# Last phase of a hybrid decoder block: finished rows scaled on ScalarE and GpSimd, gates in own buffers, later mean products, and projection matmuls of 512 columns

## The chip, the cores and the metric

The kernel runs on one core of a Trainium2 chip. The metric is the device time of one execution in microseconds; the time of a kernel is the median of its runs. TensorE (PE) multiplies, with its weight loads (PEld) beside; VectorE (DVE), ScalarE (ACT) and GpSimd (POOL) do the rest, and all transfers here are issued by SyncE (SP), in order.

## The reference

One decoder block with two token mixers over 2048 tokens of 1024 channels, in float32, cut to what matters here:

```python
h = _rmsnorm(x, norm_g) * (1 + scale) + shift
p = h @ w_in                       # c_val, c_gate, c_og, r/k/v/loras, r_og, g_conv, g_rwkv
y_conv = (silu(LN(conv31(c_val * sigmoid(c_gate)))) * silu(c_og)) @ w_conv_out
y_rwkv = (groupnorm(rwkv7_scan(...)) + bonus) * silu(r_og) @ w_rwkv_out
m = sigmoid(g_conv) * y_conv + sigmoid(g_rwkv) * y_rwkv
x = x + gate * (m @ w_out)
return _rmsnorm(x, final_g)
```

## The kernel before, in words

**Number format.** Each product that must be exact to float32 is made of three fp32r matmuls: both operands are split into a high part (a cast on ScalarE) and a low part (a subtraction, on VectorE or GpSimd), and hi x hi, hi x lo and lo x hi are added up in PSUM. `mm3k` (L316) writes the three for one of the eight 128-row slices of the contraction. A result tile is 128 channels x 512 tokens; `MS` (L44) says into how many matmuls its 512 columns are divided, two here, each with its own weight load.

**Stages.** Tokens go in four blocks of 512. The main phase makes, for each block, 73 tiles of the input projection (`product`, L959), the convolution (31 multiply-adds on VectorE, L997), and the delta-rule scan in eight pairs of heads (`pair`, `group`, `inverse`, `merge`), whose 128x512 matmuls L616 to L622 share TensorE's queue with the projections. It leaves convolution rows `y`, scan rows `o`, and the gates (tanh values in `gr_d`, `gc_d`) in DRAM. The last phase begins at about 2283 us and runs for each block `pb` through 8 tiles of the scan branch's output (`rjob`), 8 of the convolution's (`cjob`), and the output product (`ojob`, four column blocks `cb`).

**Beside them** run side chains. `z_first` adds and gates scan rows. `lnorm_first` makes the channel layer norm of `y`: part 0 adds up eight tiles (L1050), then a product with a matrix of ones gives the mean (L1060); part 1 subtracts it (L1069), squares (L1071) and adds (L1078), then a product gives the variance (L1086); part 2 normalises, multiplies by the gate and stores `u` (L1088 to L1107). Some of their operations go to `other()`: GpSimd, or VectorE once all convolution rows of the kernel are made. `hprep` loads `z` or `u` rows and splits them for the next stage (L492, L493).

**The take of a tile.** In `rjob`, L1304 reads a finished PSUM tile with the gate `rth` into `mr`; in `cjob`, L1318 and L1319 do so for the other branch, and L1336 and L1337 split the sum for `ojob`. There are two PSUM buffers for these tiles, so a product's matmuls wait until the take of the second tile before it is done. The gate lies in a ring of two buffers (`t2`), which it shares with the squares of `ojob` (L1380).

**The end of a block.** In `ojob`, L1379 adds the x rows, L1381 sums squares, and `norm` makes the reciprocal root in twelve small VectorE operations and then scales: eight L1392 for a block, VectorE, each followed by a store to `out` (L1394). The tiles of x that are scaled are used again: block 0's by the `mr` tiles of block 1, the others' by the x rows of the next block. Weights of the last phase come split from DRAM, or raw (`raw`, L285 to L291) with the split made on the spot: for the scan branch in blocks 2 and 3, for the convolution branch in blocks 1 to 3.

**Order.** PE's order is written by a planner: each matmul adds its planned time to a clock, jobs follow one another, and threads (side chains, scan) come in when their condition holds and a delay has passed (`yield (condition, delay)`). `late_free` asks whether the one PSUM bank of the side chains is free. The other engines' instructions are put in order by the framework, from its own estimate of times; `tc.high_priority` moves some forward.

Of the kernel before, what the change touches and what calls it, by code (L numbers as in the profile page):

```python
# [9 lines left out]
F32 = mybir.dt.float32  # L10
F32R = mybir.dt.float32r
I32 = mybir.dt.int32
AF = mybir.ActivationFunctionType
ALU = mybir.AluOpType
# [4 lines left out]
P = 128  # L19
D = 1024  # L20
KT = D // P
TB = 512
NTT = TB // P
CH = 64
NCH = TB // CH
# [5 lines left out]
BKB, T2B, OCB = 1, 2, 2  # L31
# [9 lines left out]
OE, LE, CE = 0, 0, 1  # L41
WLL = 1
TRE = 1
MS, MS2 = 2, 1  # L44
WB = 7
OPAD, MOFF = 64, 16
KEPT = ("in",)
# [24 lines left out]
LLD, LST, LDA, LLA, LPO, LDT, LAS, LT1 = 8.0, 3.0, 4.0, 5.0, 36.0, 5.0, 6.0, 3.0  # L72
LOOK, DUO, NHF, LHF, LYJ = 13, 2, 9, 5.0, 34.0
LOOK3, LSD = 80, 2.6
NPB = 4
# [14 lines left out]
def hybrid_block(ctx: ExitStack, tc: tile.TileContext, x, vecs, convk, w2a2, final_g, ada, w_in, w_co, w_ro, w_o, crow, out,  # L90
                 seq=2048, groups=(0, 1, 2, 3), phase2=True, dbg=None):
    nc = tc.nc
# [187 lines left out]
    def load_w(name, n, hl=None, held=None, raw=False):  # L280
        if hl is None:
            hl = [whl.tile([P, KT, P], F32R, name=n_, tag="w", bufs=WB) for n_ in ("w_hi", "w_lo")]
        hi, lo = hl
        back = kept.get((name, n))
        if raw:  # L285
            st = l3.tile([P, KT, P], F32, name="w_raw", tag="tk", bufs=TKB)
            nc.sync.dma_start(st, wsrc[name][n])
            with tc.high_priority(HP):
                nc.scalar.copy(hi, st)
                (nc.gpsimd if name == "ro" and n < 2 else nc.vector).tensor_tensor(out=lo, in0=st, in1=hi.bitcast(F32), op=ALU.subtract)  # L290
            return hi, lo  # L291
        if back is not None:
            nc.sync.dma_start(hi.bitcast(F32), back[0].bitcast(F32))
            nc.sync.dma_start(lo.bitcast(F32), back[1].bitcast(F32))
            return hi, lo
        st = whl.tile([P, KT, P], F32, name="w_st", tag="w", bufs=WB)
        ada_ld[0] = nc.sync.dma_start(st, wsrc[name][n]).ins
        wcount[0] -= 1
        with tc.high_priority(HP):
            nc.scalar.copy(hi, st)  # L300
            lo_eng = nc.vector if wcount[0] >= 0 or (wcount[0] < -1000 and wcount[0] % 4 < W2) else nc.gpsimd
            lo_eng.tensor_tensor(out=lo, in0=st, in1=hi.bitcast(F32), op=ALU.subtract)  # L302
        if name in KEPT:
            i = "_".join(str(k) for k in (n if isinstance(n, tuple) else (n,)))
            def store():
                kept[(name, n)] = [dp.tile([P, KT, P], F32R, name=f"k{p_}_{name}{i}", tag=f"k{p_}_{name}{i}") for p_ in "hl"]
                nc.sync.dma_start(kept[(name, n)][0].bitcast(F32), hi.bitcast(F32))
                nc.sync.dma_start(kept[(name, n)][1].bitcast(F32), lo.bitcast(F32))

            if held is None:  # L310
                store()
            else:
                held.append(store)
        return hi, lo
# [59 lines left out]
    e1 = early.enter_context(tc.tile_pool(name="e1", bufs=1, side="right"))  # L374
    xp = early.enter_context(tc.tile_pool(name="xp", bufs=HXB, side="right"))
    hp = early.enter_context(tc.tile_pool(name="hp", bufs=1, side="right"))
    e2 = early.enter_context(tc.tile_pool(name="e2", bufs=2, side="right"))
# [658 lines left out]
    def lnorm_first(pb, part):  # L1036

        def yload(j):
            yj = hx("lny")
            behind(nc.sync.dma_start(yj, y_dram[pb][j]))  # L1040
            return yj

        if part == 0:
            yield (free, 1.0)
            ys, n_ = yload(0), [yload(1), yload(2)]
            yield LLD
            for j in range(1, KT):
                yield (free, 0.0)
                item(1)
                behind(other().tensor_tensor(out=ys, in0=ys, in1=n_.pop(0), op=ALU.add))  # L1050
                if j + 2 < KT:
                    n_.append(yload(j + 2))
                yield pace(LSD)
                item(-1)
            ln0["ys"] = ys
        elif part == 1:
            n_ = [yload(0)]
            yield (late_free, 0.0)
            ps = pl.tile([P, TB], F32, name="late", tag="late")
            te(0.9).matmul(ps, ones, ln0["ys"], start=True, stop=True)  # L1060
            bank[0] = clock[0] + LCH
            ln0["mean"] = ln0["ys"]
            nc.scalar.copy(ln0["mean"], ps)
            yield LLD
            for j in range(KT):
                yield (free, 0.0)
                item(1)
                yj = n_.pop(0)
                behind(nc.gpsimd.tensor_tensor(out=yj, in0=yj, in1=ln0["mean"], op=ALU.subtract))  # L1069
                yield pace(1.5)  # L1070
                behind(nc.scalar.activation(yj, yj, AF.Square))  # L1071
                if j + 1 < KT:
                    n_.append(yload(j + 1))
                yield pace(1.5)
                if j == 0:
                    qs = yj
                else:
                    behind(other().tensor_tensor(out=qs, in0=qs, in1=yj, op=ALU.add))  # L1078
                yield pace(LSD / 2)
                item(-1)  # L1080
            ln0["qs"] = qs
        else:
            qs = ln0["qs"]
            yield (late_free, 0.0)
            ps = pl.tile([P, TB], F32, name="late", tag="late")
            te(0.9).matmul(ps, ones, qs, start=True, stop=True)  # L1086
            bank[0] = clock[0] + LCH
            nc.vector.tensor_scalar(out=qs, in0=ps, scalar1=LN_EPS, scalar2=None, op0=ALU.add)  # L1088
            ln0["rl"] = hx("lnr")
            rsqrt(ln0["rl"], qs, None, nc.vector, hx("lnt"))  # L1090
            n_ = [yload(0)]
            yield LLD
            for j in range(KT):
                yield (free, 0.0)
                item(1)
                yj, ct = n_.pop(0), hx("lnc")
                behind(nc.sync.dma_start(ct, co_dram[pb][j]))
                behind(nc.gpsimd.tensor_tensor(out=yj, in0=yj, in1=ln0["mean"], op=ALU.subtract))  # L1098
                other().tensor_tensor(out=yj, in0=yj, in1=ln0["rl"], op=ALU.mult)
                yield pace(LST)  # L1100
                swish_y(yj, hx("lnth"), j)
                if j + 1 < KT:
                    n_.append(yload(j + 1))
                yield pace(LST)
                behind(other().tensor_tensor(out=yj, in0=yj, in1=ct, op=ALU.mult))
                yield pace(LST)
                behind(nc.sync.dma_start(u_dram[pb][j], yj))  # L1107
                item(-1)
# [183 lines left out]
    w4 = {}  # L1292
    mtags = ["M", "ta", "E2", "k", "sq", "r", "sh", "lw"]

    def whole(name):
        return l3.tile([P, 2, 2, NCH, P], F32R, name=name, tag="As", bufs=2).rearrange(
            "p q h c t -> p (q h) (c t)").rearrange("p a (b t) -> p (a b) t", t=TB)

    def rjob(b, n):
        def take(ppr):  # L1300
            mr0 = w4.setdefault(("mr", b), [])
            mr0.append(e1.tile([P, TB], F32, name="mr0", tag=mtags[n]))
            with tc.high_priority(HP):
                nc.vector.scalar_tensor_tensor(out=mr0[n], in0=w4.pop(("th", n)), scalar=1.0, in1=ppr, op0=ALU.add, op1=ALU.mult)  # L1304

        def run():
            w4["th", n] = th = e2.tile([P, TB], F32, name="rth0", tag="t2", bufs=T2B)
            nc.sync.dma_start(th, gr_dram[b][n])
            yield from product(n, take, -1000, "ro", b > 1)

        return [None, run(), 0]

    def cjob(b, n):
# [25 lines left out]
            m0[1].append(lo)  # L1339

        def run():
            w4["th", n] = th = e2.tile([P, TB], F32, name="cth0", tag="t2", bufs=T2B)
            nc.sync.dma_start(th, gc_dram[b][n])
            yield from product(n, take, -1000, "co", b > 0)

# [17 lines left out]
    def ojob(b, cb):  # L1363
# [19 lines left out]
        def norm(t0, t1):  # L1383
            ts_ = slice(t0, t1)
            nc.vector.tensor_reduce(out=vs[:, ts_], in_=sq4[:, ts_], axis=AX.X, op=ALU.add)
            nc.vector.tensor_scalar(out=vs[:, ts_], in0=vs[:, ts_], scalar1=1.0 / D, scalar2=RMS_EPS, op0=ALU.mult, op1=ALU.add)
            rsqrt(rs[:, ts_], vs[:, ts_], None, nc.vector, rt[:, ts_])
            for tt in range(t0, t1):
                for half in range(2):
                    hs = slice(half * TB, half * TB + TB)  # L1390
                    xt = xts0[4 * half + tt]
                    nc.vector.scalar_tensor_tensor(out=xt, in0=xt, scalar=rs[:, tt:tt + 1], in1=w4["fg"][:, hs],  # L1392
                                                   op0=ALU.mult, op1=ALU.mult)
                    nc.sync.dma_start(out[b * TB + tt * P:b * TB + tt * P + P, hs], xt)  # L1394

        for kh, tt in [(kh, tt) for tt in range(NTT) for kh in range(2)] if end else [(kh, tt) for kh in range(2) for tt in range(NTT)]:
# [129 lines left out]
```

## Time and profile before

| | us |
|---|---|
| median of 3 runs | 2896.63 (2895.95 to 2897.0) |
| the profiled execution | 2893.5 |
| its span, first to last instruction | 2891.8 |
| PE busy in it, weight loads | 2767.5, 2677.1 |
| VectorE, GpSimd, ScalarE busy | 1998.4, 1338.6, 1017.5 |
| mean granted TensorE clock | 0.986 |

The profile is of one execution. Rows of groups have: line, engine, operation, tiles written and read, shapes, count, then the busy time in all and the mean in ns of one, then the idle time of the engine just before them and what ended it. Rows of the timeline have the start and the length in us, and idle time ahead of the row in brackets. Rows by stage have the stretch, its length, busy time (and count) of PE, PEld, DVE, ACT and POOL, the granted clock, the DMA engines' share and GB/s.

### The profile page before, as it was taken

The numbers are of one execution on the slowest core, as the hardware profiler recorded it, in microseconds if no ns is written. First come the engines' busy times: TensorE is split into PE (matmuls) and PEld (weight loads), VectorE is DVE, ScalarE is ACT, GpSimd is POOL, SyncE is SP. The second block draws the span as 40 slices with busy tenths as digits, with TensorE's granted clock in tenths as the row PEclk, the third lists the DMA queues.
The fourth block names the chain that finished last, engine by engine and source line by source line (L and its number), as shares of the span: only waits on it lengthen the run. The fifth ranks groups of instructions, "written<-read, shape, count | busy, mean of one in ns | idle before, by whom it ended". The sixth has DMA issues, their size and how long they took to land.

```text
span 2891.8 us, 67549 instructions
## 1 busy us (share of the span) xinstructions
PE 2767.5 (96%) x27184; PEld 2677.1 (93%) x27184; DVE 1998.4 (69%) x3453; ACT 1017.5 (35%) x1994; POOL 1338.6 (46%) x1996
## 2 busy tenths in 40 slices
PE   6989999999999999999999999999999999998998
PEld 6988999899999999999999988999999989898998
DVE  6694886767677787768587768586857465666353
ACT  5443334433433324343333343324332233333221
POOL 2447554843555344556455746676665440230000
PEclk9999999999999999999999999999999999999999
DMA  8776877766887776868886667866696779797664
GB/s 316 261 254 216 282 248 243 262 226 216 278 281 250 262 259 199 285 213 252 272 250 212 219 203 225 304 213 229 218 309 206 244 245 331 258 345 261 208 215 161
DMA packets 376971, 717.75 MB, mean 248 GB/s; under 512 B 130833, under 2 KB 149585, under 8 KB 376658
## 3 DMA queue, kind: packets, MB, share of 16 engines
q1 hardware_dynamic: 376658, 713.44, 73.4%
q8 instruction: 214, 3.51, 0.5%
q14 instruction: 99, 0.81, 0.1%
HBM read 511.91 MB, written 200.29 MB: 246 GB/s over the span
## 4 chain that ended last, share of the span: by engine, by line
PE 58%; DVE 11%; DMA 7%; POOL 4%; issue 2%; ACT 1%; SPq 1%; DVEq 0%; POOLq 0%; ACTq 0%
PE ps_main L323 41%; DVE acc L997 3%; PE pout L1403 2%; PE pout L1405 2%; PE pout L1404 2%; PE xo L882 2%; DMA lny<-y_d 2%; PE xo L876 1%; PE aux L692 1%; PE xo L889 1%; DMA w_st<-w_in_t 1%; DMA As<-dT 1%; POOL TT L776 1%; POOL itmp L772 1%; DVE h_lo L493 1%
## 5 line engine op out<-in xcount | busy, mean ns | idle before, releaser
L323 PE MATMUL ps_main<-h_hi,w_hi 128*128 128x256 f32 x5632 | 1173.5, 290 | 29.7 <-DVE mr L1304 13.8
L323 PE MATMUL ps_main<-h_hi,w_lo 128*128 128x256 f32 x5632 | 1111.7, 279 | 2.7 <-POOL w_lo L302 2.1
L323 PE MATMUL ps_main<-h_lo,w_hi 128*128 128x256 f32 x5632 | 1112.8, 279 | 0.0
L323 PEld LDWEIGHTS ps_main<-h_hi,w_hi 128*128 128x128 f32 x5632 | 862.2, 190 | 61.0 <-DVE mr L1304 8.5
L323 PEld LDWEIGHTS ps_main<-h_hi,w_lo 128*128 128x128 f32 x5632 | 860.1, 190 | 3.3 <-POOL w_lo L302 2.6
L323 PEld LDWEIGHTS ps_main<-h_lo,w_hi 128*128 128x128 f32 x5632 | 862.5, 190 | 0.0
L997 DVE SCALAR_TENSOR_TENSOR acc<-u,ck,acc 128x512 f32<-128x512 f32 x928 | 698.4, 753 | 19.5
L772 POOL TENSOR_TENSOR itmp<-La,TT 128x126 f32<-128x126 f32 (+22 forms) x496 | 190.4, 384 | 68.4 <-DMA La<-dA 35.6
L776 POOL TENSOR_TENSOR TT<-TT,itmp 128x126 f32<-128x126 f32 (+22 forms) x496 | 197.2, 398 | 34.6
L302 POOL TENSOR_TENSOR w_lo<-w_st,w_hi 128x1024 fp32r<-128x1024 f32 x51 | 123.6, 2424 | 183.9 <-ACT w_hi L300 170.4
L893 DVE TENSOR_TENSOR S<-xo,Se 64x128 f32<-64x128 f32 x256 | 73.4, 287 | 138.7 <-PE xo L889 131.6
L871 ACT ACTIVATE Se<-S,pe 128x128 f32<-128x128 f32 x256 | 88.9, 395 | 223.1 <-DVE S L893 222.1
L1403 PE MATMUL pout<-w_hi,m_hi 128*128 128x256 f32 x512 | 145.1, 283 | 1.0 <-DVE xt L1379 1.0
L1404 PE MATMUL pout<-w_lo,m_hi 128*128 128x256 f32 x512 | 143.9, 281 | 0.0
L1405 PE MATMUL pout<-w_hi,m_lo 128*128 128x256 f32 x512 | 143.9, 281 | 0.0
L300 ACT CAST w_hi<-w_st 128x1024 fp32r<-128x1024 f32 x71 | 74.4, 1048 | 166.0 <-DMA w_st<-w_in_t 127.3
L884 DVE TENSOR_TENSOR uv<-xo,rn 64x256 f32<-64x256 f32 x128 | 53.7, 420 | 103.5 <-PE xo L882 101.9
L493 DVE TENSOR_TENSOR h_lo<-hf,h_hi 128x512 fp32r<-128x512 f32 x96 | 78.0, 829 | 64.0 <-ACT h_hi L492 63.8
L660 POOL TENSOR_TENSOR ta<-ta,k 128x512 f32<-128x512 f32 x32 | 46.4, 1449 | 131.5 <-ACT ta L659 131.4
L575 ACT ACTIVATE t<-ps_main,mu 128x512 f32<-128x512 f32 x96 | 65.6, 684 | 114.9 <-PE ps_main L323 112.6
L1098 POOL TENSOR_TENSOR lny<-lny 128x512 f32<-128x512 f32 x32 | 45.0, 1407 | 116.2 <-DMA lny<-y_d 87.8
L1403 PEld LDWEIGHTS pout<-w_hi,m_hi 128*128 128x128 f32 x512 | 96.5, 189 | 1.7 <-DVE xt L1379 1.4
(257 smaller groups left out, 4247.9 us busy)
## 6 DMA issues: line engine op xcount, KB each, us to landing
w_hi<-kh_in SPq DMA_DIRECT2D x219, 512.0 KB, 5.6
w_lo<-kl_in SPq DMA_DIRECT2D x219, 512.0 KB, 4.1
w_st<-w_in_t SPq DMA_DIRECT2D x73, 512.0 KB, 4.7
kh_in<-w_hi SPq DMA_DIRECT2D x71, 512.0 KB, 2.9
kl_in<-w_lo SPq DMA_DIRECT2D x71, 512.0 KB, 4.1
lny<-y_d SPq DMA_DIRECT2D x96, 256.0 KB, 5.6
w_hi<-kh_o SPq DMA_DIRECT2D x32, 512.0 KB, 6.2
w_lo<-kl_o SPq DMA_DIRECT2D x32, 512.0 KB, 5.5
```

The lines of the kernel that those rows point to most:

```text
L300: nc.scalar.copy(hi, st)
L302: lo_eng.tensor_tensor(out=lo, in0=st, in1=hi.bitcast(F32), op=ALU.subtract)
L323: lastpe[0] = te(0.113 * 2 / ms).matmul(ps[:, qs], ww[:, k, :], aa[k][:, qs], start=(k == 0 and t == 0 and q == 0), stop=(k == KT - 1 and ...
L493: nc.vector.tensor_tensor(out=lo, in0=src, in1=hi.bitcast(F32), op=ALU.subtract)
L772: first = nc.gpsimd.tensor_tensor(out=tmp[:, :ni, :nt], in0=La[:, j:j + 1, j + 1:].broadcast_to([P, ni, nt]), in1=TT[:, :ni, j:j + 1].broa ...
L776: nc.gpsimd.tensor_tensor(out=TT[:, :ni, j + 1:], in0=TT[:, :ni, j + 1:], in1=tmp[:, :ni, :nt], op=ALU.add)
L871: nc.scalar.mul(Se[:, q, :], Sg[:, q, :], R[q]["pe"][:, c:c + 1])
L893: nc.vector.tensor_tensor(out=Sg[hs, :, hs], in0=xo[hs, 2:4, hs], in1=Se[hs, :, hs], op=ALU.add)
L997: nc.vector.scalar_tensor_tensor(out=acc if i + 1 < HALO else yj, in0=u[:, i:i + TB], scalar=ck[:, j, i:i + 1], in1=acc, op0=ALU.mult, op1 ...
L1403: te(0.113).matmul(o_, m0[0][kk][:, ts_], whi[:, k, :], start=st_, stop=False, skip_group_check=True)
L1404: te(0.113).matmul(o_, m0[0][kk][:, ts_], wlo[:, k, :], start=False, stop=False, skip_group_check=True)
L1405: lastpe[0] = te(0.113).matmul(o_, m0[1][kk][:, ts_], whi[:, k, :], start=False, stop=(kk == KT - 1), skip_group_check=True).ins
```

## The change

1. `MS` goes from 2 to 1: each L323 matmul has 512 columns, and one weight load where there were two.
2. The gates of the last phase get buffers outside the ring for blocks 1 to 3 (`thtile`): the scan's tiles `E1` and `la` in turn.
3. In blocks 0 to 2 the finished rows are scaled by ScalarE and multiplied by `final_g` on GpSimd; the last block stays on VectorE.
4. The two mean products of the layer norm wait for a planner delay of `LLD`, 8 us, behind the free bank.
5. The low parts of the first two raw scan weights of blocks 2 and 3 are made by VectorE, not GpSimd.

```diff
-MS, MS2 = 2, 1
+MS, MS2 = 1, 1
...
-                (nc.gpsimd if name == "ro" and n < 2 else nc.vector).tensor_tensor(out=lo, in0=st, in1=hi.bitcast(F32), op=ALU.subtract)
+                nc.vector.tensor_tensor(out=lo, in0=st, in1=hi.bitcast(F32), op=ALU.subtract)
...
-            yield (late_free, 0.0)
+            yield (late_free, LLD)
             ps = pl.tile([P, TB], F32, name="late", tag="late")
             te(0.9).matmul(ps, ones, ln0["ys"], start=True, stop=True)
...
-            yield (late_free, 0.0)
+            yield (late_free, LLD)
             ps = pl.tile([P, TB], F32, name="late", tag="late")
             te(0.9).matmul(ps, ones, qs, start=True, stop=True)
...
+    def thtile(b, n):
+        if not b:
+            return e2.tile([P, TB], F32, name="th0", tag="t2", bufs=T2B)
+        if n % 2:
+            return e1.tile([P, TB], F32, name="th1", tag="la")
+        return e1.tile([P, NCH, CH + 1], F32, name="th1", tag="E1", bufs=1).rearrange("p a b -> p (a b)")[:, :TB]
...
-            w4["th", n] = th = e2.tile([P, TB], F32, name="rth0", tag="t2", bufs=T2B)
+            w4["th", n] = th = thtile(b, n)
...
-            w4["th", n] = th = e2.tile([P, TB], F32, name="cth0", tag="t2", bufs=T2B)
+            w4["th", n] = th = thtile(b, n)
...
-                    nc.vector.scalar_tensor_tensor(out=xt, in0=xt, scalar=rs[:, tt:tt + 1], in1=w4["fg"][:, hs],
-                                                   op0=ALU.mult, op1=ALU.mult)
+                    if b + 1 < NPB:
+                        nc.scalar.activation(xt, xt, AF.Identity, scale=rs[:, tt:tt + 1])
+                        nc.gpsimd.tensor_tensor(out=xt, in0=xt, in1=w4["fg"][:, hs], op=ALU.mult)
+                    else:
+                        nc.vector.scalar_tensor_tensor(out=xt, in0=xt, scalar=rs[:, tt:tt + 1], in1=w4["fg"][:, hs],
+                                                       op0=ALU.mult, op1=ALU.mult)
```

Lines of the changed kernel stand up to 11 further down: its L1311 is L1304 of before, its L1325, L1326 and L1344 are L1318, L1319 and L1337. The scaling on ScalarE is L1400 and the product on GpSimd L1401.

How the order moves, first on VectorE, at the end of block 1's output product. Before, from the last small operation of the norm (`small`) on; `xt` are finished rows, `mr` the take of a tile of block 2, `w_lo` low parts of raw weights:

```order
L141 SCALAR_TENSOR_TENSOR small_33808<-small_33808 128x4
L1392 SCALAR_TENSOR_TENSOR xt_33796<-xt_33796,small_33808,fg_34287 128x512
L1392 SCALAR_TENSOR_TENSOR xt_33802<-xt_33802,small_33808,fg_34287 128x512
L1392 SCALAR_TENSOR_TENSOR xt_33796<-xt_33796,small_33808,fg_34287 128x512
L1392 SCALAR_TENSOR_TENSOR xt_33802<-xt_33802,small_33808,fg_34287 128x512
L1392 SCALAR_TENSOR_TENSOR xt_33799<-xt_33799,small_33808,fg_34287 128x512
L1392 SCALAR_TENSOR_TENSOR xt_33805<-xt_33805,small_33808,fg_34287 128x512
L1392 SCALAR_TENSOR_TENSOR xt_33799<-xt_33799,small_33808,fg_34287 128x512
L1392 SCALAR_TENSOR_TENSOR xt_33805<-xt_33805,small_33808,fg_34287 128x512
L1099 TENSOR_TENSOR lny<-lny,lnr 128x512
L1304 SCALAR_TENSOR_TENSOR mr_34548<-rth_34440,ps_main 128x512
L290 TENSOR_TENSOR w_lo<-w_raw,w_hi 128x1024 x2
```

And the same place in the changed kernel, where `th` is the gate:

```order
L141 SCALAR_TENSOR_TENSOR small_25974<-small_25974 128x4
L1099 TENSOR_TENSOR lny<-lny,lnr 128x512
L1311 SCALAR_TENSOR_TENSOR mr_26692<-th_26614,ps_main 128x512
L1311 SCALAR_TENSOR_TENSOR mr_26706<-th_26626,ps_main 128x512
L290 TENSOR_TENSOR w_lo<-w_raw,w_hi 128x1024 x2
L333 SCALAR_TENSOR_TENSOR lny<-lnth,lny 128x512
L1311 SCALAR_TENSOR_TENSOR mr_26753<-th_26714,ps_main 128x512
```

The eight scalings are gone from VectorE's queue; on GpSimd eight L1401 stand between the third and the fourth L1098 of the last block's layer norm. Then on TensorE, around the last block's mean product, before (`late` is the side chains' bank, `xo` the scan's):

```order
L323 MATMUL ps_main<-h_hi,w_hi 128x256 x2
L323 MATMUL ps_main<-h_lo,w_hi 128x256 x2
L323 MATMUL ps_main<-h_hi,w_lo 128x256 x2
L1060 MATMUL late<-lny,ones 128x512
L889 MATMUL xo<-uv,tk 128x128 x2
```

and in the changed kernel:

```order
L323 MATMUL ps_main<-h_hi,w_hi 128x512
L323 MATMUL ps_main<-h_lo,w_hi 128x512
L323 MATMUL ps_main<-h_hi,w_lo 128x512
L1060 MATMUL late<-lny,ones 128x512
L323 MATMUL ps_main<-h_hi,w_hi 128x512
```

The two rows of 256 columns have become one of 512 everywhere. The product has moved out of the scan's last chain: 309.5 weight tiles of L323 stand ahead of it in the old order and 318.4 in the new, and the part of the layer norm behind it has moved with it. Nothing else on TensorE changes its place by more than a few instructions but the other mean products and the scan matmuls next to them.

## The prediction

> **What bounds the kernel now.** I read the page first: busy times, then the costliest groups.
>
> ```profile
> PE 2767.5 (96%) x27184; PEld 2677.1 (93%) x27184; DVE 1998.4 (69%) x3453; ACT 1017.5 (35%) x1994; POOL 1338.6 (46%) x1996
> ...
> PE 58%; DVE 11%; DMA 7%; POOL 4%; issue 2%; ACT 1%; SPq 1%; DVEq 0%; POOLq 0%; ACTq 0%
> ...
> L323 PE MATMUL ps_main<-h_hi,w_hi 128*128 128x256 f32 x5632 | 1173.5, 290 | 29.7 <-DVE mr L1304 13.8
> L323 PE MATMUL ps_main<-h_hi,w_lo 128*128 128x256 f32 x5632 | 1111.7, 279 | 2.7 <-POOL w_lo L302 2.1
> L323 PE MATMUL ps_main<-h_lo,w_hi 128*128 128x256 f32 x5632 | 1112.8, 279 | 0.0
> ```
>
> TensorE is busy for 96% of the span and has the most of the chain that ended last. Its work is line L323: 16,896 matmuls of 256 columns (with 192 more under another name at the start, 17,088, or 8,544 pairs of 512 columns). So two things can move the time: what a pair costs, and the idle time between them. The mean durations (279 to 290 ns) overlap, so a matmul's price is the step from one start to the next. The timeline of PE gives it, with two starts in each row; these are the first and last rows of two stretches without a break, 48 rows apart each:
>
> ```profile
> 2678.77 0.39 PE L323 MATMUL ps_main<-h_hi,w_hi 128*128 128x256 f32 x2
> ...
> 2689.65 0.39 PE L323 MATMUL ps_main<-h_hi,w_hi 128*128 128x256 f32 x2
> ```
> ```profile
> 2626.26 0.40 PE L323 MATMUL ps_main<-h_hi,w_hi 128*128 128x256 f32 x2
> ...
> 2637.57 0.40 PE L323 MATMUL ps_main<-h_hi,w_hi 128*128 128x256 f32 x2
> ```
>
> The first makes 10.88 us / 48 = 226.7 ns for a pair, the second 11.31 / 48 = 235.6. The same instructions run at two rates, and a stretch keeps its rate until something interrupts it. Counted over the whole trace, 15,652 steps between L323 matmuls run unbroken at full clock: 11,801 take 115 ns or less, 3,851 take 116 to 126. Their mean is 114.6, so **229.2 ns for a pair today**.
>
> For the idle time I read the last phase (2283 us to the end), which most of the edits touch. The same timeline marks idle time ahead of a row in brackets; these are its three largest gaps after 2440 us:
>
> ```profile
> 2457.81 1.13 PE L1060 MATMUL late<-lny,ones 128*128 128x512 f32 x2 [3.63 <-DVE lny L1050]
> ```
> ```profile
> 2505.02 0.77 PE L323 MATMUL ps_main<-h_hi,w_hi 128*128 128x256 f32 x2 [4.52 <-DVE mr L1304]
> ```
> ```profile
> 2618.18 0.58 PE L323 MATMUL ps_main<-h_hi,w_hi 128*128 128x256 f32 x1 [6.50 <-DVE mr L1304]
> ```
>
> Each ends with VectorE. At 2618 a PSUM buffer has to be freed by L1304, which stands behind eight L1392 in VectorE's queue:
>
> ```profile
> 2610.46 6.47 DVE L1392 SCALAR_TENSOR_TENSOR xt<-xt,small,fg 128x512 f32<-128x512 f32 x8
> ...
> 2616.85 0.68 DVE L1099 TENSOR_TENSOR lny<-lny,lnr 128x512 f32<-128x512 f32 x1
> 2617.45 0.67 DVE L1304 SCALAR_TENSOR_TENSOR mr<-rth,ps_main 128x512 f32<-128x512 f32 x1
> ```
>
> The table by stage (us, busy times by engine, granted clock, DMA) shows what follows such a gap:
>
> ```profile
> 2618.20:2626.30 8.10, 8.10 (x49) 8.10 (x50) 4.71 (x7) 1.93 (x3) 0.00 (x0) 0.68 1.02 381
> ...
> 2673.00:2700.00 27.00, 27.00 (x241) 27.00 (x240) 12.32 (x16) 5.21 (x7) 0.00 (x0) 1.00 0.53 181
> ```
>
> The clock granted is 0.68 behind the gap and 1.00 elsewhere: 8.1 x 0.32 = 2.6 us lost after the gap itself.
>
> **The change part by part.** *512 columns for each L323 matmul.* It takes away 8,544 matmuls and as many weight loads, and streams as many columns as before. The nearest rows are the 128x512 matmuls of the pair threads, of the same type, one weight load each. In the timeline of PE:
>
> ```profile
> 1325.06 0.40 PE L616 MATMUL aux<-lw,wl 128*128 128x512 f32 x1
> ...
> 1326.00 0.41 PE L323 MATMUL ps_main<-h_hi,w_hi 128*128 128x256 f32 x2
> ```
> ```profile
> 1201.65 0.39 PE L621 MATMUL aux<-la,wl 128*128 128x512 f32 x1
> 1201.88 0.39 PE L622 MATMUL aux<-la,wlo 128*128 128x512 f32 x1
> 1202.11 0.40 PE L323 MATMUL ps_main<-h_hi,w_hi 128*128 128x256 f32 x2
> ```
>
> Four of them take 0.94 us (235 each) in the first place, two take 0.46 (230 each) in the second; the 93 steps behind L617, L621 and L622 at full clock, which these rows begin and end, run from 227 to 239 but for one (248), with a mean of 234. So no 512-column step is cheaper than the quick pair, 226.7, and most lie near the slow one, 235.6: the price goes with the columns, in the same two rates. The term lies between -2.5 x 8,544 = -21 us (every stretch at 226.7) and (234 - 229.2) x 8,544 = +41 us (every stretch at that mean). I take 0: the rate is chosen where a stretch begins, the interruptions stay where they are, and so should the mix. The short rows, all from the head of a stretch, say less of a long one.
>
> The Trainium skill, page "TensorE: Matmul & The Clock Gate", section "Back-to-back issue gap", has N / 2.4 + 2.5 ns between warm matmuls, which would make 109.2 for 256 columns and 215.8 for 512. The trace does not agree with either figure (113.3 and 230 to 235), but the fixed part would be saved 8,544 times; by it the term is an estimated -21 us.
>
> *Finished rows on ScalarE and GpSimd.* 24 of the 32 L1392 leave VectorE (0.78 us each, 18.7 us in three lots of eight); the last block keeps its own. In their place come 24 scalings on ScalarE and 24 products on GpSimd. The nearest rows, groups by line:
>
> ```profile
> L1392 DVE SCALAR_TENSOR_TENSOR xt<-xt,small,fg 128x512 f32<-128x512 f32 x32 | 22.9, 781 | 0.2
> ...
> L332 ACT ACTIVATE lny<-lny,v 128x512 f32<-128x512 f32 x32 | 26.0, 813 | 0.7
> ...
> L1133 POOL TENSOR_TENSOR z<-z 128x512 f32<-128x512 f32 x8 | 11.4, 1430 | 18.9 <-DMA z<-bv_d 18.8
> ```
>
> A lot becomes 0.8 + 8 x 1.43 = 12.2 us on GpSimd, where it took 6.5. ScalarE (35% busy) holds each lot for 8 x 0.81 = 6.5 us, ahead of the casts of raw weights, which run up to three tiles (16 us) early. The stores of `out` come up to 6 us later on SP's queue and hold up the gate and weight loads behind them; the x rows that reuse the buffers are wanted a block later. What it buys: in the DVE order only one L1099 is left ahead of the first L1304, so at 2618 that would have run by about 2611.2 and not 2617.45; the gap of 6.5 us and the 2.6 us of slow clock go: **-9 us**.
>
> What it costs is traffic with GpSimd. VectorE and POOL rows of the same moments:
>
> ```profile
> 2497.37 0.71 DVE L493 TENSOR_TENSOR h_lo<-hf,h_hi 128x512 fp32r<-128x512 f32 x1
> 2498.46 3.60 DVE L493 TENSOR_TENSOR h_lo<-hf,h_hi 128x512 fp32r<-128x512 f32 x2 [0.38 <-ACT h_hi L492]
> ```
> ```profile
> 2497.61 2.23 POOL L938 TENSOR_TENSOR uv<-uv,grs 128x1024 f32<-128x1024 f32 x1
> 2499.81 3.39 POOL L1069 TENSOR_TENSOR lny<-lny 128x512 f32<-128x512 f32 x2
> ```
>
> An h_lo takes 0.71 us alone and 1.8 beside a GpSimd product: 1.1 us more. Eight L1401 in a row can put off VectorE by up to 8 x 1.1 = 9 us a lot, 27 us in three, at worst all on PE; at best nothing, since PE is two products ahead. The nearest stretch, 2491 to 2505 (two such meetings and a gap of 4.5 us), makes me take +1 us a lot, **+3 us**. The Trainium skill, page "SBUF — State Buffer", section "Who interferes with whom", speaks against this edit: a VectorE operation with two SBUF inputs and a GpSimd operation that reads SBUF exclude each other for the whole instruction. The trace agrees (0.71 against 1.8 us).
>
> *Gates in own buffers* (`E1` and `la` in place of the ring shared with the squares): the loads need not wait for the squares of the norm. L1304 waited 2.3 us for its gate in the whole run:
>
> ```profile
> L1304 DVE SCALAR_TENSOR_TENSOR mr<-rth,ps_main 128x512 f32<-128x512 f32 x32 | 21.8, 681 | 7.3 <-PE ps_main L323 4.9 <-DMA rth<-gr_d 2.3
> ```
>
> So 0 to -2, taken as 0. *Mean products later*: in PE's order that of the last block moves from 1.5 weight tiles behind block 0's output product to 10.4 (48 us at 5.4 a tile), and the sum that it waits for moves less far: **-3.6 us**. The layer norm slips by some nine products (50 us); its u rows are wanted in the last block only. Nine of its operations go from GpSimd to VectorE, 9 x 0.69 us, beside matmuls. *Low parts of four weight tiles on VectorE*: 1.25 us each, up to three tiles early: 0.
>
> The middle gap, 4.5 us at 2505 with 12 x 0.28 = 3.4 us of slow clock behind it, is VectorE's order and those meetings:
>
> ```profile
> 2500.00:2512.00 12.00, 7.48 (x43) 7.31 (x42) 9.01 (x10) 4.08 (x6) 3.19 (x2) 0.72 0.58 196
> ```
>
> After the change seven sums (L1050) stand there instead of L1078, and the GpSimd subtractions are elsewhere. Between 0 and -7.9 I take half, **-4**.
>
> The sum: 0 - 9 + 3 - 3.6 - 4 = -13.6 us. The profiled execution took 2893.5 us (span 2891.8 and 1.7 around it), 3.1 below the median of 2896.63; the difference carried to the median gives **2883 us**.
>
> **The rivals.** *A, 512 columns stay at the slower rate.* For it: the 93 steps, mean 234. Against: some of them take 227 to 230, and the 256-column stretches are quick three times in four. Price: +41, of which I let a tenth fall into waits, +37, so 2920. It decides as soon as a matmul's mean step passes 229.2 + 13.6 / 8.544 = 230.8 ns. *B, the fixed part is saved, or every stretch is quick*: 226.7 for each, -21, so 2862; against it, no 512-column row shows less than 227. This is where the page's rule, an estimate, also ends. *C, the last phase gives its gain back*: GpSimd's lots hold up VectorE by 9 us each where only one gap is saved; -13.6 becomes about 0, so 2897. For it the rows of 2498; against it, L1304 itself keeps its 0.68 us and suffers only behind others. That the change doesn't do what it says is not open: the order shows 128x512 in every L323 row.
>
> **How the numbers follow.** My forecast 0.43, A 0.28, B 0.19, C 0.10. A measurement of this kernel tells 0.2% (5.8 us) from no change. Faster: 0.38 of the forecast and B's 0.19 = 0.57. Same: the rest of the forecast (0.05) and most of C (0.08) = 0.13. Slower: A and the rest of C = 0.30. The range takes in B, with 3 us for a better middle gap, and A to its edge: 2860 to 2922. The likeliest case alone, with the middle gap and the GpSimd meetings at both ends, is 2874 to 2892.
>
> **What would show it.** Right: L323 steps of 227 and 235 ns side by side with a mean near 229; no gap over 2 us behind a block's norm or ahead of L1060. Wrong: a mean step over 231 or under 227 (the first term); the eight L1401 with h_lo and L290 at twice their time and a PE gap behind them (the +3).

## The result and the profile after

The changed kernel takes **2929.93 us** (2924.13 to 2932.8, four runs) against 2896.82 (2895.95 to 2898.17): a ratio of 1.0111, 95% interval 1.0094 to 1.0129. That is 33 us slower, 47 above the forecast of 2883 and 8 above the upper end of the range. The profiled execution has a span of 2921.6 us and is the fastest of the four.

The page's busy times and its costliest groups, of the changed kernel:

```profile
PE 2801.2 (96%) x18640; PEld 2270.0 (78%) x18640; DVE 1999.9 (68%) x3442; ACT 1032.4 (35%) x2018; POOL 1352.5 (46%) x2007
...
L323 PE MATMUL ps_main<-h_hi,w_hi 128*128 128x512 f32 x2816 | 1177.6, 418 | 30.0 <-DVE mr L1311 7.2
L323 PE MATMUL ps_main<-h_lo,w_hi 128*128 128x512 f32 x2816 | 1121.2, 398 | 1.0 <-DVE h_lo L493 1.0
L323 PE MATMUL ps_main<-h_hi,w_lo 128*128 128x512 f32 x2816 | 1120.3, 398 | 1.7 <-POOL w_lo L302 1.2
```

TensorE is busy for 34 us more with 8,544 matmuls fewer (2801.2 against 2767.5), and its weight loads for 407 us less, which buys nothing. The price of a matmul is the step between starts again. In the timeline of PE, the first and the last row of an unbroken stretch, 48 matmuls apart:

```profile
2640.69 0.39 PE L323 MATMUL ps_main<-h_hi,w_hi 128*128 128x512 f32 x1
...
2651.89 0.40 PE L323 MATMUL ps_main<-h_hi,w_hi 128*128 128x512 f32 x1
```

11.20 us / 48 = **233.3 ns**. It is so everywhere: of the 6,201 steps that lie in unbroken stretches at full clock, 6,061 are in stretches whose mean rounds to 233.0 or 233.5, and no stretch has a mean below 231.5. Within a stretch the steps are either all 233 or 231 and 236 in turn, with the same mean. The two rates of before, 226.7 and 235.6 for a pair, have become one that is near the slower.

The last phase has hardly changed in sum: 617.1 us before (2274.7 to 2891.8), 617.4 after. By stage it has. The table by stage, cut at the first matmul of each, before and after: block 1's scan branch, its convolution and output, block 2's scan branch, its convolution and output.

```profile
2444.60:2505.02 60.42, 51.51 (x485) 49.69 (x483) 36.08 (x63) 15.41 (x28) 19.93 (x22) 0.99 0.85 315
2505.02:2600.60 95.58, 95.03 (x778) 94.31 (x779) 66.74 (x92) 32.94 (x65) 24.36 (x15) 0.97 0.84 306
2600.60:2655.73 55.13, 47.86 (x387) 47.31 (x385) 34.56 (x53) 17.23 (x26) 4.05 (x3) 0.94 0.81 291
2655.73:2746.03 90.30, 90.00 (x769) 89.60 (x770) 36.57 (x56) 24.91 (x54) 4.80 (x2) 1.00 0.60 201
```
```profile
2475.30:2531.80 56.50, 51.80 (x279) 40.78 (x277) 30.52 (x58) 17.10 (x28) 20.22 (x24) 0.97 0.94 359
2531.80:2628.80 97.00, 95.31 (x589) 84.23 (x590) 68.59 (x88) 31.76 (x66) 24.98 (x17) 0.98 0.87 305
2628.80:2675.30 46.50, 45.22 (x195) 35.69 (x193) 33.23 (x46) 23.25 (x34) 19.81 (x13) 1.00 0.94 335
2675.30:2773.55 98.25, 93.19 (x577) 82.43 (x578) 47.69 (x69) 30.19 (x62) 3.39 (x3) 0.98 0.63 214
```

The third row is the forecast gain: 55.13 became 46.50 us and the clock went from 0.94 to 1.00. The fourth gives it back: PE was busy for 90.00 of 90.30 us and is now for 93.19 of 98.25. Its gaps are new, in the timeline of PE:

```profile
2684.63 0.50 PE L323 MATMUL ps_main<-h_hi,w_hi 128*128 128x512 f32 x1 [2.05 <-ACT h_hi L492]
...
2694.38 0.50 PE L323 MATMUL ps_main<-h_hi,w_hi 128*128 128x512 f32 x1 [1.53 <-DVE th L1325]
```

So there were two questions for the runs: whether the width carries the 33 us, and what the other edits are worth without it.

### The profile page after: what moved, and what is told of

Same layout as the page of the kernel before. It is cut to its first block, busy times and chain, and to the rows that moved or that the text cites. A ratio compares the mean times of both kernels' runs of the same rounds, so it can differ in the third digit from the quotient of the medians.

```text
span 2921.6 us, 50494 instructions
## 1 busy us (share of the span) xinstructions
PE 2801.2 (96%) x18640; PEld 2270.0 (78%) x18640; DVE 1999.9 (68%) x3442; ACT 1032.4 (35%) x2018; POOL 1352.5 (46%) x2007
## 5 line engine op out<-in xcount | busy, mean ns | idle before, releaser
L323 PE MATMUL ps_main<-h_hi,w_hi 128*128 128x512 f32 x2816 | 1177.6, 418 | 30.0 <-DVE mr L1311 7.2
L323 PE MATMUL ps_main<-h_lo,w_hi 128*128 128x512 f32 x2816 | 1121.2, 398 | 1.0 <-DVE h_lo L493 1.0
L323 PE MATMUL ps_main<-h_hi,w_lo 128*128 128x512 f32 x2816 | 1120.3, 398 | 1.7 <-POOL w_lo L302 1.2
L323 PEld LDWEIGHTS ps_main<-h_hi,w_hi 128*128 128x128 f32 x2816 | 534.9, 190 | 165.3 <-ACT carry L581 8.5
L323 PEld LDWEIGHTS ps_main<-h_hi,w_lo 128*128 128x128 f32 x2816 | 534.3, 190 | 132.3 <-POOL w_lo L302 1.7
L323 PEld LDWEIGHTS ps_main<-h_lo,w_hi 128*128 128x128 f32 x2816 | 536.0, 190 | 106.1 <-DVE h_lo L493 1.7
L772 POOL TENSOR_TENSOR itmp<-La,TT 128x126 f32<-128x126 f32 (+22 forms) x496 | 188.5, 380 | 64.1 <-DMA La<-dA 30.6
L882 PEld LDWEIGHTS xo<-XO,As 64*64 64x64 f32 x1024 | 69.7, 135 | 48.1 <-issue 27.1
L705 POOL TENSOR_TENSOR BK<-BK,pe 128x1024 f32<-128x1024 f32 x32 | 63.5, 1985 | 84.3 <-PE aux L692 73.5
```

Source lines behind the costliest of these rows:

```text
L323: lastpe[0] = te(0.113 * 2 / ms).matmul(ps[:, qs], ww[:, k, :], aa[k][:, qs], start=(k == 0 and t == 0 and q == 0), stop=(k == KT - 1 and ...
L772: first = nc.gpsimd.tensor_tensor(out=tmp[:, :ni, :nt], in0=La[:, j:j + 1, j + 1:].broadcast_to([P, ni, nt]), in1=TT[:, :ni, j:j + 1].broa ...
```

## The experiments

Each is compared with the kernel before on the same chip. One profiled execution differs from the next by several us in the main phase, so times are taken from the ratios and stages from the profiles.

**The width alone.**

```diff
-MS, MS2 = 2, 1
+MS, MS2 = 1, 1
```

> The kernel before with MS = 1 and nothing else: every L323 matmul 128x512. Theory T (the width term alone made the changed kernel slower: its full-clock steps have a mean of 233.3 ns, where a pair of 256 columns cost 229.2): + 4.1 x 8,544 = +35 us, so 2932 us, main phase about 29 us longer, full-clock mean step 233.3 with no stretch near 227. The prediction's term (the mix of rates stays): 0, so 2897 us. Rival G (something of the other edits in the main phase, such as gates, mean products or more slow clock, carries a good part): 2897 plus less than 25 us.

Measured: ratio 1.0096 (1.0082 to 1.011), 2928.4 against 2897.96 us: +28 by the ratio. The full-clock step is 233.3 ns. The prediction's zero is excluded. The 35 us of the steps come out as 28 (24 to 32). Most of the other 7 can be placed: some 580 times a stretch begins behind an interruption, and there the first 512-column step takes 320 ns where the first two of 256 take 325 (206 and 119). That is 5 ns less instead of 4 more, 5 us in all, and leaves 30, which lies in the interval.

**The other edits without the width** (the changed kernel with MS = 2).

> The changed kernel with MS = 2, all its other edits kept. Theory T: the last phase took 617.1 us before and 617.4 after, of which 1,536 x 4.1 = +6.3 us are the width, so the rest is worth -6: 2891 us. The prediction's sum: -13.6, so 2883 us, without the gaps at 2618, 2505 and 2458 us of before. Rival C of the prediction (the last phase gives its gain back): 2897 us. Rival G: slower than 2897 in the main phase as well.

Measured: 1.0023 (1.0014 to 1.0033), 2903.98 us: +7, where the prediction had -14 and this theory -6. All were wrong, C (+0) by least; that a part of the 7 lies in the main phase (rival G) is not excluded. 1.0096 x 1.0023 = 1.0119 against 1.0111 for both: the two halves of the change add up.

**What makes the quick rate.** Two kernels keep 256 columns and write the same six matmuls in another order:

```diff
-        for t, (ww, aa) in enumerate(((whi, ahi), (whi, alo), (wlo, ahi))):
-            for q in range(ms):
...
+        for t, q in ((0, 0), (1, 0), (2, 0), (0, 1), (1, 1), (2, 1)):
```

> The kernel before, 256 columns, but the three products of one half follow one another before the other half's three: two of three steps stay in the same 256 columns of PSUM. Theory S (a step is quick, 113.3 ns, only where consecutive matmuls write different columns of PSUM, and slow, 117.7, where they add to the same ones): the pair goes from 229.2 to between 232.5 (two steps in three slow) and 235.4 (all slow), +28 to +53 us, 2925 to 2950 us. Rival N (512 columns in one instruction are what costs 233.3, whatever is written): no change, 2897 us with quick and slow stretches as before. Rival W (quick only where the next load brings the weights that are already in place): half the pairs of equal weights are left, +10 to +30 us.

```diff
+        for t, q in ((0, 0), (1, 1), (2, 0), (0, 1), (1, 0), (2, 1)):
```

> The kernel before, 256 columns, halves still in turn, but the products staggered so that w_hi, w_hi, w_lo, w_hi, w_hi, w_lo follow one another and the second of two equal loads has other data: no step stays in the same columns of PSUM. Theory S: as before, 2897 us, quick and slow stretches both there. Rival N: 2897 us too. Rival W (equal weights in a row make the quick step): weights change in two steps of three where they changed in two of six, so about half of the quick steps are lost, +15 to +30 us.

Measured: 1.0024 (1.0015 to 1.0034) and 1.0017 (1.0006 to 1.0027), +7 and +5 us. In the first, three matmuls in a row add to the same columns, and both rates are there all the same; the timeline of PE, two stretches of 96 steps (L324 is L323 of before):

```profile
2536.03 0.28 PE L324 MATMUL ps_main<-h_lo,w_hi 128*128 128x256 f32 x1
...
2547.34 0.28 PE L324 MATMUL ps_main<-h_lo,w_hi 128*128 128x256 f32 x1
```
```profile
2634.44 0.28 PE L324 MATMUL ps_main<-h_hi,w_lo 128*128 128x256 f32 x1
...
2645.32 0.28 PE L324 MATMUL ps_main<-h_hi,w_lo 128*128 128x256 f32 x1
```

11.31 / 96 = 117.8 and 10.88 / 96 = 113.3 ns. The mean of the full-clock steps is 114.4 in this kernel and 114.6 in the other, against 114.6 before. Theory S falls (it wanted 28 us at least), and so does W: neither the columns written nor the order of the weights decides. What is left is the width itself, N. The 5 to 7 us are not rate, and where they lie is not known. They are not in the first steps of the stretches either: without 7 to 11 steps of over 300 ns in each kernel, the mean of these some 580 steps is 206 ns before and 205 in both kernels here.

**A quarter of the width.**

```diff
-MS, MS2 = 2, 1
+MS, MS2 = 4, 1
```

> The kernel before with MS = 4: 128 columns in each L323 matmul, four weight loads where there were two. If the step goes with the columns as between 256 and 512 (113.3 or 117.7, and 233.3): 57 to 59 ns, 227 to 235 for 512 columns, 2880 to 2950 us. If a weight load sets a floor (PEld is busy for 98 ns for each of today's loads): about 98 ns a step, 392 for 512 columns, +1,390 us, so 4,290 us. Between the two, the step itself is what is looked for.

Measured: 1.6939 (1.6877 to 1.7), 4907.72 us in two runs, longer than either forecast. The timeline of PE has four starts in each row, one row after the other:

```profile
1400.43 0.61 PE L323 MATMUL ps_main<-h_hi,w_lo 128*128 128x128 f32 x4
1400.88 0.61 PE L323 MATMUL ps_main<-h_hi,w_hi 128*128 128x128 f32 x4
1401.32 0.61 PE L323 MATMUL ps_main<-h_lo,w_hi 128*128 128x128 f32 x4
```

0.89 us / 8 = 111 ns for 128 columns (30,400 of its 33,575 steps lie between 100 and 118, with a mean of 111.7), nearly as much as for 256. By that step the kernel loses (4 x 111.7 - 229.2) x 8,544 = 1,860 us of the 2,009 measured. So 128 columns cost what 256 do, as if there were a floor of about 112 ns; the quick rate at 256 sits under 2 ns above it. No other width below 256 was run. The Trainium skill, page "TensorE: Matmul & The Clock Gate", section "Back-to-back issue gap", has N / 2.4 + 2.5 ns for a matmul by itself, an estimated 55.8 ns for 128 columns, and about 81 ns at 128 columns and 131 at 512 for a stream of weight loads and matmuls; the runs here agree with neither (111.7 at 128, 113.3 or 117.7 at 256, 233.3 at 512). What sets the floor, a weight load or these operands, was not tried apart.

**The other edits one by one**, all with 256 columns. First the later mean products alone, at both places:

```diff
-            yield (late_free, 0.0)
+            yield (late_free, LLD)
```

> The kernel before with the later mean products alone (LLD at both places). The changed kernel with MS = 2 was 6.6 us slower than before where the prediction's sum had -13.6; in its last phase the gap at 2618 us was gone (the stage lost 9.9 us), but two later stages were 5.4 and 8.9 us longer. Theory L (the delay moves the last block's layer norm among the convolution branch's tiles of blocks 1 and 2, where VectorE's takes of PSUM stand behind its steps that wait for GpSimd): +8 to +14 us, 2906 to 2912, with gaps ahead of L323 that end on L1318 in these stages. Theory G (GpSimd's scalings give the gain back): the prediction's -3.6, 2894. Theory I (each edit gains alone and they meet badly): -3.6.

Then the finished rows on ScalarE and GpSimd alone (the last hunk of the change):

> The kernel before with the finished rows on ScalarE and GpSimd alone. Theory L: the prediction's -9 + 3 = -6 us and a part of the middle gap, 2888 to 2892. Theory G: 0 to +6 us, 2898 to 2904, since VectorE waits for GpSimd and the stores of out hold up SyncE's queue. Theory I: -6 us.

The changed kernel without the delay, and the changed kernel with the finished rows on VectorE:

> The changed kernel with MS = 2 and without the delay of the mean products (finished rows, gates and low parts as changed). Theory L: without its cause the loss goes, and the gaps at 2618 and 2505 us stay closed: -6 to -10 us, 2888 to 2892. Theory G: 0 to +6 us, 2898 to 2904. Theory I: -6 to -10.

> The changed kernel with MS = 2 and the finished rows on VectorE as before (later mean products, gates and low parts as changed). Theory L: the gap at 2618 us is back and the loss of the later stages is there too: +10 to +16 us, 2908 to 2914. Theory G: the loss goes with GpSimd's products: -4 to -8 us, 2890 to 2894. Theory I: -4.

And with neither, only the gates and the low parts:

> The kernel before with only the gates in own buffers and the four low parts on VectorE. In the profiles, the finished rows on GpSimd alone left 4.0 us of the gap of 6.5 at 2618 us, because the low parts of block 2's first weights stood behind the eight products on GpSimd; with these two edits beside, the gap was gone (stage of 46.5 us against 52.3 and 55.1 before). Theory Q (the two edits do nothing by themselves and only remove that wait): 0 to -2 us, 2897 to 2899, stage of block 2's scan branch near 55 us. Rival (they gain by themselves what lies between the runs with the finished rows alone and with all three): -6 us, 2893.

Together with the run above they make a table of two edits, ratios with their intervals (gates and low parts as changed, but for the runs of the second line):

| | rows on VectorE | rows on ScalarE and GpSimd |
|---|---|---|
| mean products as before | 0.9993 (0.9981 to 1.0004) | 0.9991 (0.9978 to 1.0003) |
| same, gates and low parts as before | 1 | 1.0014 (1.0001 to 1.0028) |
| mean products later | 1.0036 (1.0022 to 1.005) | 1.0023 (1.0014 to 1.0033) |

The delay costs 0.0043 with the rows on VectorE and 0.0032 without, 12 and 9 us, and 5 us by itself (1.0017, 1.0004 to 1.0029); each of the three is known to 4 or 5 us, so they can't be told apart. That is theory L in sign, and in size with the rows on VectorE (+10 us against before, forecast +10 to +16); by itself the delay costs less than L's +8 to +14. G, which blamed GpSimd's products, falls for the delay, and so does I, since no edit gains alone. But L's other half falls too: without the delay the finished rows gain nothing that is clear of zero (-0.6 us between the two runs of the first line), and by themselves they cost 4 us, as G had it. Gates and low parts alone change nothing, as theory Q had it; block 2's scan stage takes 54.8 us with them.

What the delay does in block 1 is in VectorE's queue. In the run with it alone, the timeline of VectorE in block 1's convolution branch, and the gap that it leaves on PE:

```profile
2547.66 1.18 DVE L1134 TENSOR_TENSOR z<-z 128x512 f32<-128x512 f32 x1
2548.77 1.78 DVE L1319 SCALAR_TENSOR_TENSOR mr<-cth,mr 128x512 f32<-128x512 f32 x1
2550.47 0.68 DVE L1078 TENSOR_TENSOR lny<-lny 128x512 f32<-128x512 f32 x1
2551.23 1.59 DVE L1337 TENSOR_TENSOR m_lo<-mr,m_hi 128x512 fp32r<-128x512 f32 x1
2552.75 0.68 DVE L1134 TENSOR_TENSOR z<-z 128x512 f32<-128x512 f32 x1
2553.35 0.68 DVE L1318 SCALAR_TENSOR_TENSOR cth<-cth,ps_main 128x512 f32<-128x512 f32 x1
```
```profile
2554.17 0.47 PE L323 MATMUL ps_main<-h_hi,w_hi 128*128 128x256 f32 x2 [2.73 <-DVE cth L1318]
```

The take L1318 stands behind two side operations, L1134 and L1078, and behind L1319 and L1337, which take 1.78 and 1.59 us here, beside GpSimd's L1133 and L1069, and 0.69 each at their next turn, 5 us on. Before, this stage had no gap above 0.6 us on PE. The squares of the last block's layer norm and their sums (L1071, L1078), which were in block 1's scan branch, have come here. In the profiles of all three runs of 256 columns with the delay this stage, with the output behind it, takes 98.7 to 101.0 us, and 94.9 to 95.6 in those without; block 2's takes 94.4 and 97.0 against 90.3 and 91.2 with the rows on VectorE, and 99.2 against 95.6 and 96.9 with the rows of all blocks on ScalarE and GpSimd. In block 2's a gap of 2.2 to 2.5 us in each of the three ends with a cast L492, which waited for u rows, and in two of them another of 2.2 and 2.9 us ends with the take.

Nor is the gap that the delay closes a gain. PE no longer waits ahead of L1060 at the beginning of block 1's scan branch, but 3 to 4 us later in the same stage it now waits for 3.1 to 3.9 us in each of the three runs. In the changed kernel with 256 columns, on PE and on VectorE:

```profile
2472.50 0.77 PE L323 MATMUL ps_main<-h_hi,w_hi 128*128 128x256 f32 x2 [3.88 <-issue]
```
```profile
2466.81 1.77 DVE L1099 TENSOR_TENSOR lny<-lny,lnr 128x512 f32<-128x512 f32 x1 [2.43 <-POOL lny L1098]
2470.30 1.17 DVE L333 SCALAR_TENSOR_TENSOR lny<-lnth,lny 128x512 f32<-128x512 f32 x1 [1.73 <-ACT lny L332]
...
2471.73 0.67 DVE L1311 SCALAR_TENSOR_TENSOR mr<-th,ps_main 128x512 f32<-128x512 f32 x1
```

The take L1311, which ends 0.1 us before PE goes on, stands behind two steps of another layer norm that wait for GpSimd and ScalarE. In the two runs with the rows on VectorE most of the wait there is for block 0's finished rows.

The stages don't hold the whole cost. Block 0's scan branch is 1.7 to 4.4 us longer with the delay, and the scan branches of blocks 1 and 2 are 1.3 to 4.1 shorter. In all, the delay makes the last phase 5.9 us longer by itself, 3.1 with the rows on ScalarE and GpSimd and 2.0 with only gates and low parts beside it, where the ratios have 5, 9 and 12. What is missing of the 9 and 12 would have to lie in the main phase, or in the choice of the profiled executions; which of the two stays open.

**The finished rows of block 1 alone** (gates and low parts as changed, no delay):

```diff
-                    if b + 1 < NPB:
+                    if b == 1:
                         nc.scalar.activation(xt, xt, AF.Identity, scale=rs[:, tt:tt + 1])
```

> The kernel before with gates and low parts as changed and the finished rows of block 1 alone on ScalarE and GpSimd (blocks 0, 2, 3 on VectorE). With blocks 0 to 2 moved, the profiles showed block 2's scan stage 8.6 us shorter, block 1's scan stage 3.6 longer (its gap before L1304 grew from 4.5 to 9.9 us) and block 2's convolution and output stage 6.6 longer (the loads of u rows stood later in SyncE's queue). Theory P (each loss belongs to the lot ahead of it): -8.6 + 6.6 = -2, 2897 us, block 1's stage near 60.5. Rival (the losses come from the reordering as such, whichever lot moves): 2 to 4 us slower, 2901 to 2903, with block 1's stage at 62 to 64 again.

Measured: 0.9998 (0.9988 to 1.0007), no change, as theory P had it. It differs from the run with gates and low parts by one lot of eight rows, so the stages show what a lot does. Block 2's two stages in the table by stage, that run first, then this one:

```profile
2611.58:2666.39 54.81, 47.73 (x387) 47.19 (x385) 33.93 (x52) 16.64 (x23) 3.87 (x3) 0.94 0.80 274
2666.39:2757.62 91.23, 90.89 (x768) 90.49 (x769) 38.02 (x58) 25.03 (x54) 0.00 (x0) 1.00 0.61 206
```
```profile
2609.11:2655.52 46.41, 44.59 (x387) 44.05 (x385) 32.06 (x42) 20.10 (x31) 18.10 (x11) 1.00 0.89 316
2655.52:2750.97 95.45, 93.40 (x768) 92.39 (x769) 39.34 (x60) 25.75 (x56) 0.00 (x0) 0.98 0.59 201
```

-8.4 us in the first stage, the forecast's -9, and +4.2 in the second. The two ratios differ by 1 us, known to 4, so about 4 more are lost or the profiles are not the typical executions; the one with gates and low parts is the slowest of its twelve, 9 us over their median. It was not settled which. Block 1's scan stage takes 62.9 us, not the 60.5 of theory P; but it takes 62.0 in the run with gates and low parts too, where no rows move. The second stage's loss has its place in SyncE's queue. The run with the finished rows alone shows it, and this run has the loads in the same order: loads of u rows (L509) and of raw weights (L287), and the gaps on PE behind them:

```profile
2648.11 3.14 SPq L509 DMA_DIRECT2D hf<-u_d  x3
2655.58 0.33 SPq L287 DMA_DIRECT2D w_raw<-w_co_t  x1
...
2657.31 0.33 SPq L287 DMA_DIRECT2D w_raw<-w_co_t  x1
...
2658.51 6.84 SPq L509 DMA_DIRECT2D hf<-u_d  x2
```
```profile
2664.33 0.50 PE L323 MATMUL ps_main<-h_hi,w_hi 128*128 128x256 f32 x2 [1.35 <-ACT h_hi L492]
...
2669.84 0.67 PE L323 MATMUL ps_main<-h_hi,w_hi 128*128 128x256 f32 x2 [1.99 <-ACT h_hi L492]
```

And the same place before:

```profile
2647.56 5.81 SPq L509 DMA_DIRECT2D hf<-u_d  x4
2654.99 0.33 SPq L287 DMA_DIRECT2D w_raw<-w_co_t  x1
...
2656.72 0.33 SPq L287 DMA_DIRECT2D w_raw<-w_co_t  x1
...
2657.92 0.32 SPq L509 DMA_DIRECT2D hf<-u_d  x1
```

Four loads of u rows stood ahead of the two raw weights, now three do; the last one goes out 6 us later, and PE waits for its cast. No store or product of the lot is in the way at that moment: the queue's written order has changed.

One reading in the expectations was wrong. The gap of 3.7 us that the finished rows alone left at 2631 us was put down to low parts behind the eight products on GpSimd. GpSimd's timeline in that run has its last low part done by 2602.1 us, long before the lot:

```profile
2599.49 2.65 POOL L290 TENSOR_TENSOR w_lo<-w_raw,w_hi 128x1024 fp32r<-128x1024 f32 x1 [1.37 <-ACT w_hi L289]
...
2614.57 5.05 POOL L1394 TENSOR_TENSOR xt<-xt,fg 128x512 f32<-128x512 f32 x4 [2.04 <-ACT xt L1393]
...
2620.84 7.89 POOL L1394 TENSOR_TENSOR xt<-xt,fg 128x512 f32<-128x512 f32 x4
```

What held the take there was VectorE's queue, beside the second half of that lot:

```profile
2623.59 2.31 DVE L290 TENSOR_TENSOR w_lo<-w_raw,w_hi 128x1024 fp32r<-128x1024 f32 x1
2625.83 1.78 DVE L333 SCALAR_TENSOR_TENSOR lny<-lnth,lny 128x512 f32<-128x512 f32 x1
2627.53 2.28 DVE L290 TENSOR_TENSOR w_lo<-w_raw,w_hi 128x1024 fp32r<-128x1024 f32 x1
2629.74 0.68 DVE L1105 TENSOR_TENSOR lny<-lny,lnc 128x512 f32<-128x512 f32 x1
2630.34 1.27 DVE L1304 SCALAR_TENSOR_TENSOR mr<-rth,ps_main 128x512 f32<-128x512 f32 x2
2631.53 1.21 DVE L290 TENSOR_TENSOR w_lo<-w_raw,w_hi 128x1024 fp32r<-128x1024 f32 x1
```

An L290 takes 2.3 us beside GpSimd's products and 1.2 without: the meeting that the prediction priced at 1.1 us an operation. The trace agrees in kind with the Trainium skill, page "SBUF — State Buffer", section "Who interferes with whom", by which a VectorE operation with two SBUF inputs contends with a GpSimd operation that reads SBUF. ScalarE's scalings had a part too: an earlier low part, at 2619.8 us, had waited 2.4 us for its cast, which stood behind the eight scalings. With gates and low parts changed too, the take stands elsewhere in that queue and the gap is gone; which of the two edits moved it was not tried.

## Why the prediction was wrong, point by point

| term | forecast, us | measured, us | from |
|---|---|---|---|
| 512 columns | 0 (-21 to +41) | +28 | the width alone |
| mean products later | -3.6 | +9 (5 by itself, 12 with the rows on VectorE) | with against without the delay |
| finished rows, gates, low parts, middle gap | -10 | -3 (finished rows alone: +4) | 0.9991 and 1.0014, without the delay |
| sum | -13.6 | +33 | the changed kernel |

- **512 columns.** The step that failed is "the rate is chosen where a stretch begins, the interruptions stay where they are, and so should the mix". There is no mix at 512 columns: one rate, 233.3 ns, in every stretch. The rows quoted against the zero had it right, 93 steps with a mean of 234. They were set aside because some took 227 to 230; but single steps scatter (231 and 236 in turn) about one mean, and only a mean over a stretch is a rate. Rival A named the mechanism; its 41 us of steps were 35, and 28 in the time.
- **Mean products.** The gap at 2457.8 us did go, but 3.1 to 3.9 us of waiting came back 3 to 4 us later in its stage, and what the delay does further on was costed at nothing: "the layer norm slips by some nine products; its u rows are wanted in the last block only". Nobody waits for its rows, but its sums and products stand in VectorE's queue ahead of the takes, and these are waited for. The cost that the traces show was in who stands behind the moved instructions, not in who needs them; they do not place the whole 9 us.
- **Finished rows.** -9 for the gap at 2618 us was right in place and size (-8.4 and -8.6 in two pairs of profiles, both with gates and low parts changed; -2.8 with the rows alone). The +3 for GpSimd's traffic was paid in the run with the rows alone (the gap of 3.7 us at 2631 us), but not with gates and low parts beside. What came back in every run without the delay, 4 to 7 us in block 2, came through SyncE's queue, where the text had the late stores hold up loads and put no price on it. Rival C had the outcome, but not this cause.
- **The middle gap.** It was to lose 4 us because other operations would stand there, which is the delay's doing, so the runs with the delay decide. The gap itself is 2.6, 4.0 and 3.6 us in the three with 256 columns and 2.2 in the changed kernel, against 4.5. The stage, which held the gap at 2457.8 us too, takes 58.8, 60.0 and 58.8 us, and 56.5 in the changed kernel, against 60.4: a gain of 0.4 to 3.9 us where the two terms had 7.6. In the other runs without the delay the stage is longer, 62.0 to 64.1 us, and where block 0's rows have moved the gap is 8.7 and 9.7 us: the low part ahead of the take then waits for a u row that landed late.
- **The range** took A at 2920 and left out that A and a loss from the other edits could come together, which is what happened: 28 + 7 is 35, and the 33 lies within the intervals. Its narrower range, 2874 to 2892, is not what its terms give: the middle gap from 0 to -7.9 and the meetings from 0 to +27 make 2876 to 2911, and the width is still at zero in it.

## What to carry to other kernels

Price an instruction's new size by the mean step of unbroken stretches of that size, wherever the kernel already has them, and trust that mean over the best single step. When work is moved because nobody is in a hurry for its result, look at what stands behind it in each in-order queue that it enters: that is who pays. A gap that closes in one stage should be followed through the next two before its gain is counted.

## What the runs showed of the hardware that was not expected

The price of these matmuls, each with a weight load of its own, is not a fixed part plus a part by column: 128 columns take 111.7 ns, 256 take 113.3 or 117.7, and 512 take 233.3. From 128 to 256 the columns are nearly free, and from 256 to 512 each column costs (233.3 - 113.3) / 256 = 0.47 ns. The two rates at 256 columns do not depend on which half of the PSUM tile is written nor on the order of the weights (a mean of 114.4 and 114.6 ns in the two other orders, against 114.6); why 256 have two and 512 columns have a single rate stays open.
